# A decoder trunk on one core: VectorE turns the first mixer's latent queries, and SyncE issues the transfers of turned queries and keys

## The chip, the core and the metric

The kernel runs on one core of one Trainium2 chip. A core has TensorE (PE, matrix products), VectorE (DVE), ScalarE (ACT), GpSimd (POOL) and SyncE (SP), which issues transfers; GpSimd issues some too. The metric is the time of one execution in device microseconds (us); lower is better.

## What is computed

Two layers over 256 positions of width 1024, each a half-step feed-forward block, a mixer with three attention branches, and a second half-step block. Of the mixer, the latent attention matters here:

```python
q = (rms_norm(c_q, q_norm) @ w_uq).reshape(B, S, 8, 64 + 32)
kv = (rms_norm(c_kv, kv_norm) @ w_ukv).reshape(B, S, 8, 64 + 64)
k = concatenate([k_nope, broadcast(k_r)], -1)
q, k = rms_norm(q, gain_q), rms_norm(k, gain_k)
q = concatenate([q[..., :64], rope(q[..., 64:], pos)], -1)   # k likewise
o_mla = causal_attention(q, k, v)                            # 8 heads of 96
...
y = gate0 * (o_sb @ proj_sb) + gate1 * (o_mla @ proj_mla) + gate2 * (o_nsa @ proj_nsa)
x = x + y @ w_out
```

The other branches are a stick-breaking attention (sb) and a sparse attention (nsa), each with 8 heads too.

## The kernel before

All products are float32 in three passes: each operand is split into a rounded part and a rest (`hi` and `lo`), and TensorE does hi x hi, hi x lo and lo x hi (`mm3`, lines 588 to 590). Weights stream from memory in slabs of 128 x 1024. In a mixer `weights()` (lines 1017 to 1049) loads each of the 69 slabs in one of two ways: as two raw tiles, which ScalarE rounds (L1042) and VectorE subtracts (L1044); or, for slabs that the feed-forward block before has already split and put into memory (`early`), as four loads of finished halves (L1030, tiles `whi` and `wlo`). 10 slabs of the first mixer and 20 of the second come that way. Four slabs have room at once (`W_BUFS`), and six raw tiles (`RAW_BUFS`). All these loads are issued by SyncE, one after the other.

Inside a mixer, generators (one for each step of each branch) ask a `Planner` for engine time with estimated costs; it picks the request that could start first (with fixed offsets, `HOLDS` and `URGENCY`) and so writes down the order of TensorE, VectorE and ScalarE (`tc.manual_schedule`, lines 383 and 991). That order is kept on the chip. The order of SyncE and of GpSimd is left to the framework, which arranges each queue's instructions by its own model of when they are ready; on the chip a queue is then worked off in that order, and an instruction that waits holds up those behind it.

The latent queries and keys must stand with the 96 head dimensions on partitions before the scores. Two ways are in the code, chosen for queries (index 0) and keys (index 1) by `by_dve` (line 1260):

- TensorE: four transposes per pair of heads into a bank of the accumulator memory (lines 1707 to 1713), 16 in all.
- VectorE: `turn` (lines 1242 to 1249) transposes each 32 x 32 block of a 128 x 768 tile in place (L1245) and sends the tile in four transfers, one for each 32 partitions, to the memory tile `md` (L1247). It runs once for each half of the positions (t = 0, 1). For each pair of heads `turned` (lines 1251 to 1257) then reads three groups of 32 head dimensions back into a half tile `st` (L1255). The planner allows 6 us for the first transfers to land (line 1249) and 5 us for the second (line 1701).

Before the change, `by_dve` is `l in (1,), l in (0, 1)`: layer 0 turns its queries on TensorE and its keys on VectorE, layer 1 turns both on VectorE. `mla_T` then splits `st`, or the accumulator bank, on ScalarE and VectorE into `qk` tiles (lines 1068 and 1070), from which `mla_scores` computes the scores (lines 1731 to 1734, recorded at lines 588 to 590 as `att<-qk`). The reads of a pair may start four slabs before its scores are due, the splits two (`MLA_AT`, the gates in lines 1699, 1705, 1707 and 1725). `nsa_T`, which overwrites the buffers of the turned tiles, waits for the last of `mla_T`'s TensorE transposes (`ev_mqk`) where one of the two goes by TensorE, and for the four `turn`s where both go by VectorE (line 1890).

Half tiles (`th`, 7 of them) are shared by `st`, gates, and several steps of the other branches. SyncE also issues `zc` (L1402), a small rearranging transfer of the sparse branch, in the middle of each mixer.

Of the kernel before, what the change touches and what calls it, by code (L numbers as in the profile page):

```python
# [17 lines left out]
S = 256  # L18
# [353 lines left out]
def decoder_trunk(ctx, tc, xt_in, wts, lcon, cst, out, depth=DEPTH):  # L372
    nc = tc.nc
# [20 lines left out]
    def big_tile(name, dt=F, shape=(128, D)):  # L394
        return hp.tile(list(shape), dt, tag="hy", name=name, bufs=6)
# [552 lines left out]
    def mixer(l):  # L948
# [14 lines left out]
        def half_tile(name):  # L963
            return mp.tile([128, 512], F, tag="th", name=name, bufs=TH_BUFS)
# [277 lines left out]
        def turn(x, t, dst, n, k):  # L1242

            k = yield "V", 0.065 + 0.00116 * n, 0.15 + 0.00116 * n, (k,), ()
            nc.vector.transpose(x[:, 0:n], x[:, 0:n])  # L1245
            for i in range(4):
                nc.gpsimd.dma_start(dst[:, :, t * 128 + 32 * i:t * 128 + 32 * (i + 1)],  # L1247
                                    x[32 * i:32 * (i + 1), 0:n].rearrange("b (m a) -> b m a", a=32))
            return Tok(k.t + 6.0)

        def turned(dst, parts):

            st = half_tile("st")
            for r, m, step, c in parts:
                nc.gpsimd.dma_start(st[32 * r:32 * (r + 1), c * S:(c + 2) * S].rearrange("b (j n) -> b j n", j=2),  # L1255
                                    dst[:, m:m + step + 1:step, :])
            return st

        mq = [big_tile("mq", F, (128, 768)) for _ in range(NT)]
        by_dve = l in (1,), l in (0, 1)  # L1260
        md = [dp.tile([32, 24, S], F, tag=f"md{i}", name="md") if by_dve[i] else None for i in range(2)]
        mk = [big_tile("mk", F, (128, 768)) for _ in range(NT)]
        ev_mq, ev_mk, ev_V1 = events(NT), events(NT), events(NT)
# [36 lines left out]
        def mla_q_norm(t, ks):  # L1300
            x = mq[t].rearrange("p (h d) -> p h d", h=8)
            k = yield use_a(768, *ks, slots=(s_tmp,))
            sq = tmp()
            nc.scalar.activation(sq, mq[t], AF.Square)
            k = yield use_v(768, k)
            ss = sm.tile([128, 16], F, tag="ss", name="ss")
            nc.vector.tensor_reduce(ss[:, 0:8], sq.rearrange("p (h d) -> p h d", h=8), axis=AX.X, op=OP.add)
            s_tmp.put(k)
            k = yield use_v1(8, k)
            r = rstd(ss, 1.0 / 96, w=8)  # L1310
            k = yield use_g(2.5, k)
            k = yield use_v(768, k)
            nc.vector.tensor_tensor(x, x, r[:, 0:8, None].to_broadcast([128, 8, 96]), op=OP.mult)
            yield "-", 0.0, 0.0, (), (s_wf,)
            b = wf()[:, 0:256].rearrange("p (h d) -> p h d", h=8)
            k = yield from t_rope(x[:, :, 64:96], x[:, :, 64:96], tab["mq"], t, 8, 32, b, k)
            s_wf.put(k)
            if by_dve[0]:
                k = yield from turn(mq[t], t, md[0], 768, k)
            ev_mq[t].set(k)  # L1320
# [19 lines left out]
        def mla_k_norm(t, ak, k):  # L1340
# [28 lines left out]
            if by_dve[1]:  # L1369
                k = yield from turn(mk[t], t, md[1], 768, k)  # L1370
# [322 lines left out]
        def mla_T():  # L1693
            for p in range(4):
                srcs = (mq, ev_mq), (mk, ev_mk)
                st, land = [None] * 2, [None] * 2
                for i, (src, ev) in enumerate(srcs):
                    if by_dve[i]:
                        k = yield "-", 0.0, 0.0, (*ev, gate(MLA_AT, p, -4)), (s_th,)
                        st[i] = turned(md[i], [(e, 6 * p + e, 3, 0) for e in range(3)])  # L1700
                        land[i] = Tok(k.t + 5.0)
                T = []
                for i, (src, ev) in enumerate(srcs):
                    if by_dve[i]:
                        k = yield "-", 0.0, 0.0, (land[i], gate(MLA_AT, p, -2)), (s_qk, s_qk)
                    else:
                        k = yield use_t(4, *ev, gate(MLA_AT, p, -2), slots=(s_tp, s_qk, s_qk))
                        st[i] = tp_tile()
                        for j in range(2):
                            for t in range(NT):  # L1710
                                h = 2 * p + j
                                nc.tensor.transpose(st[i][:96, (2 * j + t) * 128:(2 * j + t + 1) * 128],
                                                    src[t][:, h * 96:(h + 1) * 96], ident)
                    if p == 3 and i == 1:
                        ev_mqk.set(k)
                    q = qk(), qk()
                    k = yield from t_split(q[0][:96], q[1][:96], st[i][:96], 512, k)
                    (s_th if by_dve[i] else s_tp).put(k)
                    T.append(q)
                    Tm[p] = T  # L1720
                    ev_Tm[p][i].set(k)
# [442 lines left out]
    for l in range(depth):  # L2164
        ffn(l, 0)
        mixer(l)
        ffn(l, 2)
# [35 lines left out]
```

## Time and profile before

| What | us |
| --- | --- |
| median of 3 runs (range) | 1248.34 (1248.22 to 1251.82) |
| the profiled execution | 1249.25 |
| its span, first to last instruction | 1247.4 |
| first mixer, first to last projection matmul | 186.6 to 422.2 |
| second mixer, likewise | 805.2 to 1041.2 |

Rows of the profile give the line of the kernel, the engine, the operation, the tiles as out<-in, and for groups the number of instructions, their busy time or their shortest, median and longest duration in ns. In a timeline the two first columns are start and duration in us, and a bracket at the end says how long the engine was idle before and what released it. SPq and POOL rows of DMA instructions are the time in which the queue is held by issuing; the time to landing is counted from the start of the issue. A matmul's end is modelled, so TensorE's true pace is read from the starts of neighbours.

### The profile page before, as it was taken

Reading aid. Unit: us, or ns where it says so; the run is one execution under the profiler, and the core shown is the slowest. Engines: PE = TensorE matmul, PEld = TensorE weight load, DVE = VectorE, ACT = ScalarE, POOL = GpSimd, SP = SyncE. Lnnn points to the kernel's source line nnn. Section 1 sums busy time; section 2 is a strip of 40 time slices with the busy share of each in tenths; the row PEclk is TensorE's granted clock in tenths of the full one; section 3 lists DMA queues with packets and bytes.
Section 4 is the critical chain, followed back from the end, with each engine's and each line's share of the span. In section 5 each row is a group of like instructions: output and inputs, shape, how many; then the busy total and the mean of one; then the engine's idle time right before and its main releaser. Section 6 shows DMA issues by size and latency. Waiting matters only on the chain.

```text
span 1247.4 us, 26169 instructions
## 1 busy us (share of the span) xinstructions
PE 1239.0 (99%) x9314; PEld 1158.8 (93%) x9314; DVE 943.6 (76%) x1961; ACT 789.0 (63%) x1633; POOL 155.5 (12%) x250
## 2 busy tenths in 40 slices
PE   9999999999999999999999999999999999999998
PEld 8999999888878899999999999998888889999987
DVE  7876668988898777766677776689968987776644
ACT  6665557787887566655465565577757775565542
POOL 0021201231000001211001121013330000023000
PEclk9999999999999999999999999999999999999999
DMA  8899985667645568999758999666896556677753
GB/s 273 288 328 327 334 270 184 196 209 245 207 126 182 158 218 260 319 322 339 233 196 272 330 328 324 213 211 191 280 323 236 159 157 185 189 211 244 220 169 119
DMA packets 157218, 298.59 MB, mean 239 GB/s; under 512 B 21472, under 2 KB 24416, under 8 KB 157088
## 3 DMA queue, kind: packets, MB, share of 16 engines
q1 hardware_dynamic: 143872, 258.64, 64.8%
q0 software_dynamic: 13216, 38.29, 8.4%
q8 instruction: 73, 1.20, 0.4%
q14 instruction: 57, 0.47, 0.1%
HBM read 258.32 MB, written 38.01 MB: 238 GB/s over the span
## 4 chain that ended last, share of the span: by engine, by line
PE 94%; ACT 2%; DVE 2%; DMA 1%; issue 1%; SPq 0%; DVEq 0%; ACTq 0%
PE acc L779 13%; PE acc L778 13%; PE acc L780 12%; PE acc L588 9%; PE acc L590 9%; PE acc L589 9%; PE acc L669 6%; PE acc L670 6%; PE acc L668 6%; PE acc L1204 1%; PE acc L1206 1%; PE acc L1205 1%; DMA raw<-in_wts 1%; PE att L2036 1%; ACT wf L1632 1%; PE tp L2047 1%
## 5 line engine op out<-in xcount | busy, mean ns | idle before, releaser
L536 DVE TENSOR_TENSOR vlo<-raw,vhi 128x512 fp32r<-128x512 f32 x452 | 292.6, 686 | 82.6 <-ACT vhi L535 80.4
L778 PE MATMUL acc<-hThi,vhi 128*128 128x256 f32 x1280 | 353.4, 276 | 0.0
L780 PE MATMUL acc<-hThi,vlo 128*128 128x256 f32 x1280 | 353.4, 276 | 0.0
L779 PE MATMUL acc<-hTlo,vhi 128*128 128x256 f32 x1280 | 353.4, 276 | 0.0
L535 ACT ACTIVATE vhi<-raw 128x512 fp32r<-128x512 f32 x452 | 263.5, 622 | 134.9 <-DMA raw<-in_wts 36.0
L778 PEld LDWEIGHTS acc<-hThi,vhi 128*128 128x128 f32 x1280 | 240.3, 188 | 0.0
L780 PEld LDWEIGHTS acc<-hThi,vlo 128*128 128x128 f32 x1280 | 240.2, 188 | 0.0
L779 PEld LDWEIGHTS acc<-hTlo,vhi 128*128 128x128 f32 x1280 | 240.2, 188 | 0.0
L1044 DVE TENSOR_TENSOR wlo<-raw,whi 128x512 fp32r<-128x512 f32 x216 | 141.1, 680 | 30.4 <-ACT whi L1042 28.7
L1042 ACT ACTIVATE whi<-raw 128x512 fp32r<-128x512 f32 x216 | 124.8, 616 | 47.6 <-PE acc L590 17.2
L670 PE MATMUL acc<-gh,vlo 128*128 128x256 f32 x528 | 145.7, 276 | 0.0
L668 PE MATMUL acc<-gh,vhi 128*128 128x256 f32 x528 | 145.7, 276 | 0.0
L669 PE MATMUL acc<-gl,vhi 128*128 128x256 f32 x528 | 145.7, 276 | 0.0
L588 PE MATMUL acc<-whi,hThi 128*128 128x512 f32 (+2 forms) x352 | 138.1, 392 | 0.0
L590 PE MATMUL acc<-whi,hTlo 128*128 128x512 f32 (+2 forms) x352 | 133.6, 380 | 0.2 <-DVE hTlo L610 0.2
L589 PE MATMUL acc<-wlo,hThi 128*128 128x512 f32 (+2 forms) x352 | 133.3, 379 | 0.0
L554 ACT ACTIVATE ehi<-eraw 128x512 fp32r<-128x512 f32 x60 | 37.9, 632 | 107.3 <-DMA eraw<-in_wts 105.1
L536 DVE TENSOR_TENSOR wlo<-raw,whi 128x512 fp32r<-128x512 f32 (+2 forms) x109 | 70.0, 678 | 45.7 <-ACT whi L535 45.5
L555 DVE TENSOR_TENSOR elo<-eraw,ehi 128x512 fp32r<-128x512 f32 x60 | 41.4, 690 | 81.0 <-ACT ehi L554 80.8
L535 ACT ACTIVATE whi<-raw 128x512 fp32r<-128x512 f32 (+2 forms) x109 | 63.1, 617 | 57.9 <-PE acc L590 26.4
L668 PEld LDWEIGHTS acc<-gh,vhi 128*128 128x128 f32 x528 | 99.1, 188 | 0.0
L669 PEld LDWEIGHTS acc<-gl,vhi 128*128 128x128 f32 x528 | 99.1, 188 | 0.0
(348 smaller groups left out, 2560.1 us busy)
## 6 DMA issues: line engine op xcount, KB each, us to landing
raw<-in_wts SPq DMA_DIRECT2D x764, 256.0 KB, 3.6
eraw<-in_wts SPq DMA_DIRECT2D x60, 256.0 KB, 5.5
early<-ehi POOLq DMA_DIRECT2D x60, 256.0 KB, 4.2
early<-elo POOLq DMA_DIRECT2D x60, 256.0 KB, 4.8
whi<-early SPq DMA_DIRECT2D x60, 256.0 KB, 4.4
wlo<-early SPq DMA_DIRECT2D x60, 256.0 KB, 4.6
st<-md POOLq DMA_DIRECT2D x36, 64.0 KB, 5.1
xd<-x SPq DMA_DIRECT2D x4, 512.0 KB, 2.6
```

Of the source, the lines that this page charges most:

```text
L535: nc.scalar.activation(hi[:, q], raw[:, o:o + g], AF.Copy)
L536: last_lo[0] = nc.vector.tensor_tensor(lo[:, q], raw[:, o:o + g], hi[:, q], op=OP.subtract).ins
L588: nc.tensor.matmul(o, a[0], b[0], start=start, stop=False, **kw)
L589: nc.tensor.matmul(o, a[0], b[1], start=False, stop=False, **kw)
L590: nc.tensor.matmul(o, a[1], b[0], start=False, stop=stop, **kw)
L668: nc.tensor.matmul(o, sl[0][:, w], h, start=k == 0 and c == 0, stop=False)
L669: nc.tensor.matmul(o, sl[0][:, w], l_, start=False, stop=False)
L670: nc.tensor.matmul(o, sl[1][:, w], h, start=False, stop=k == kts - 1 and c == 1)
L778: nc.tensor.matmul(o, sl[0][:, w], h, start=k == 0 and c == 0, stop=False)
L779: nc.tensor.matmul(o, sl[0][:, w], l_, start=False, stop=False)
L780: nc.tensor.matmul(o, sl[1][:, w], h, start=False, stop=k == KT - 1 and c == 1)
L1044: nc.vector.tensor_tensor(hl[1][:, c:c + m], raw[:, :m], hl[0][:, c:c + m], op=OP.subtract)
```

## The change

Layer 0 takes the VectorE path for its queries too, so in both layers queries and keys go through `turn` and `turned`; and all transfers of these two functions are issued by SyncE. The tile `md0` now exists in both layers, TensorE's 16 transposes of `mq` are gone, and `nsa_T` of layer 0 waits for the `turn`s in place of `ev_mqk`. For each mixer that makes 16 writes to `md` and 24 reads into `st` on SyncE's queue; before, GpSimd issued 8 and 12 of them in layer 0, 16 and 24 in layer 1. The planner is run anew with the same costs and offsets.

```diff
             nc.vector.transpose(x[:, 0:n], x[:, 0:n])
             for i in range(4):
-                nc.gpsimd.dma_start(dst[:, :, t * 128 + 32 * i:t * 128 + 32 * (i + 1)],
-                                    x[32 * i:32 * (i + 1), 0:n].rearrange("b (m a) -> b m a", a=32))
+                nc.sync.dma_start(dst[:, :, t * 128 + 32 * i:t * 128 + 32 * (i + 1)],
+                                  x[32 * i:32 * (i + 1), 0:n].rearrange("b (m a) -> b m a", a=32))
             return Tok(k.t + 6.0)
...
             for r, m, step, c in parts:
-                nc.gpsimd.dma_start(st[32 * r:32 * (r + 1), c * S:(c + 2) * S].rearrange("b (j n) -> b j n", j=2),
-                                    dst[:, m:m + step + 1:step, :])
+                nc.sync.dma_start(st[32 * r:32 * (r + 1), c * S:(c + 2) * S].rearrange("b (j n) -> b j n", j=2),
+                                  dst[:, m:m + step + 1:step, :])
             return st
...
-        by_dve = l in (1,), l in (0, 1)
+        by_dve = True, True
```

## The prediction

> **What bounds the kernel now.** The page first, for the engine whose work is the time; then the busy time of both mixers side by side, since the change touches only them.
>
> ```profile
> span 1247.4 us, 26169 instructions
> PE 1239.0 (99%) x9314; PEld 1158.8 (93%) x9314; DVE 943.6 (76%) x1961; ACT 789.0 (63%) x1633; POOL 155.5 (12%) x250
> PE 94%; ACT 2%; DVE 2%; DMA 1%; issue 1%; SPq 0%; DVEq 0%; ACTq 0%
> ```
>
> ```profile
> core 0: us, PE busy (x) PEld busy (x) DVE busy (x) ACT busy (x) POOL busy (x), PEclk, DMA share, GB/s
> 186.60:422.20 235.60, 234.86 (x1417) 200.64 (x1417) 206.80 (x523) 181.90 (x435) 28.04 (x31) 1.00 0.61 188
> 805.20:1041.20 236.00, 233.70 (x1401) 199.49 (x1400) 199.70 (x512) 171.09 (x411) 38.68 (x51) 1.00 0.69 217
> ```
>
> TensorE is busy 99% of the span and is 94% of the chain that ended last, at full clock in both mixers. So a change can win only TensorE work that goes, or TensorE idle time that closes; and it loses whatever makes TensorE wait in its fixed order. The two windows run from the first to the last projection matmul of each mixer. Layer 1 already turns queries and keys on VectorE; layer 0 turns only the keys so. Layer 1 has 16 matmuls fewer, exactly the transposes the change removes, yet it takes 0.4 us more: its TensorE idles 2.30 us (236.00 - 233.70), layer 0's 0.74. That is the nearest thing to a trial of the first half of the change, and it says: no gain. (Layer 1 also has more weights split ahead, so it is not a clean trial.)
>
> **The transposes.** Four groups of four, one per pair of heads, between projection matmuls; the row of the tile and one group in the timeline (start, duration):
>
> ```profile
> L1712 PE MATMUL tp<-ident,mq x16: 270/272/276, 278.1 to 317.1; 128*96 128x128 f32 x16
> ```
>
> ```profile
> 277.92 0.39 PE L590 MATMUL acc<-whi,hTlo 128*128 128x512 f32 x1
> 278.15 0.60 PE L1712 MATMUL tp<-ident,mq 128*96 128x128 f32 x4
> 278.50 0.48 PE L588 MATMUL acc<-whi,hThi 128*128 128x512 f32 x1
> 278.82 0.39 PE L589 MATMUL acc<-wlo,hThi 128*128 128x512 f32 x1
> ```
>
> The 272 ns each overlap; what counts is the delay of the neighbours. Projection matmuls follow each other every 0.23 us (277.92 to 278.15, where the group begins in L588's place). Without the group, L589 would start at 277.92 + 2 x 0.23 = 278.38; it starts at 278.82. So a group costs 0.44 us, four cost 1.75 us, all on the path: **-1.75 us**.
>
> **What replaces them in layer 0** is what layer 1 does now: two VectorE block transposes, 8 writes to the DRAM tile md and 12 reads back into st. The chain behind the last turn of layer 1, to the first scores, from the timelines of the engines:
>
> ```profile
> 891.72 0.97 DVE L1245 STREAM_TRANSPOSE mk<-mk 128x768 f32<-128x768 f32 x1
> 892.99 2.88 POOL L1247 DMA_DIRECT2D md<-mk  x4 [0.43 <-DVE mk L1245]
> 901.60 1.61 POOL L1255 DMA_DIRECT2D st<-md  x3 [5.74 <-ACT kd L1888]
> 908.21 0.63 ACT L1068 ACTIVATE qk<-st 96x512 fp32r<-96x512 f32 x1 [2.31 <-DMA st<-md]
> 908.01 0.28 PE L590 MATMUL acc<-whi,hTlo 128*128 128x256 f32 x1
> 908.89 0.33 PE L588 MATMUL att<-qk 96*128 96x128 f32 x1 [0.60 <-ACT qk L1068]
> 909.61 0.33 PE L589 MATMUL att<-qk 96*128 96x128 f32 x1 [0.40 <-DVE qk L1070]
> 914.57 0.39 PE L590 MATMUL acc<-whi,ol 128*128 128x512 f32 x1
> 915.64 0.33 PE L1673 MATMUL tp<-ident,wf 128*128 128x128 f32 x1 [0.68 <-ACT wf L1664]
> ```
>
> The turn ends at 892.69, the split of the read data starts at 908.21: 15.5 us, while the kernel's planner allows 6 + 5 (lines 1249 and 1701). TensorE waits: 0.76 us before the first score matmul (0.12 us is a neighbour's normal step), 0.60 before the second, 0.84 before the transposes of the probabilities: 2.2 us, nearly all of layer 1's idle time. This chain has no slack, so its changes arrive one for one.
>
> ```profile
> whi<-early SPq DMA_DIRECT2D x16, 256.0 KB, 5.1
> wlo<-early SPq DMA_DIRECT2D x16, 256.0 KB, 5.3
> raw<-in_wts SPq DMA_DIRECT2D x4, 256.0 KB, 4.6
> md<-mk POOLq DMA_DIRECT2D x8, 96.0 KB, 4.5
> st<-md POOLq DMA_DIRECT2D x12, 64.0 KB, 5.6
> zc<-wf SPq DMA_DIRECT2D x4, 64.0 KB, 4.3
> ```
>
> ```profile
> st<-md POOLq DMA_DIRECT2D x9, 64.0 KB, 3.0
> md<-mk POOLq DMA_DIRECT2D x4, 96.0 KB, 2.6
> ```
>
> These are the transfers issued in 871 to 907 (layer 1) and, in the second fence, two kinds of those in 252 to 288 (layer 0), with the median time to landing. In layer 0 a write and a read land 1.9 + 2.6 = 4.5 us sooner, more than the 2.2 us that layer 1 is late by. The new stall in layer 0 lies between 0 and 2.2 us; I take **+0.7**, nearer to nothing for that reason. VectorE's two turns are 1.94 us on an engine that is 88% busy there (206.80 of 235.60); bounds 0 and 1.9, with the planner's new order of layer 0 in it (without the transposes it may put other steps earlier, worth -0.5 to +1); I take **+0.4**, since VectorE's 12% of free time covers most of it. Where that cover is gone, the weight splits queue behind the turn, and TensorE behind them.
>
> **The move to SyncE.** Per mixer 16 writes and 24 reads go from GpSimd's queue, where nothing urgent stands behind them, to the queue that loads all weights, in order. Its prices:
>
> ```profile
> L514 SPq DMA_DIRECT2D raw<-in_wts x494: 327/328/1557, 192.6 to 1040.5; - x165
> L1402 SPq DMA_DIRECT2D zc<-wf x8: 593/608/699, 267.4 to 890.4; - x8
> L1030 SPq DMA_DIRECT2D whi<-early x16: 327/404/1069, 870.7 to 905.0; - x16
> L1030 SPq DMA_DIRECT2D wlo<-early x16: 319/355/583, 871.1 to 905.5; - x16
> L1247 POOL DMA_DIRECT2D md<-mk x16: 692/740/789, 248.9 to 895.1; - x16
> L1255 POOL DMA_DIRECT2D st<-md x36: 533/536/605, 271.9 to 924.8; - x36
> ```
>
> No row shows SyncE issuing an md write. By the code it consists of 32 x 24 = 768 runs of 128 bytes; a raw load has 128 runs and holds SyncE 0.328 us; zc, the only transfer here with short runs (64 partitions x 4), has 256 and holds it 0.608. If the hold goes by the instruction, md costs 0.33; if by the run, 0.608 + 512 x (0.608 - 0.328) / 128 = 1.73. I take 1.2, half-way up from zc, the nearest row. An st read has 64 runs, at most 0.33.
>
> The Trainium skill ("Perfetto Trace Analysis", section "DMA Instruction — HWDGE (DVE, Sync)") says that the profiled window of a SyncE DMA covers the generation of all its descriptors, after which SyncE is free. By that rule the per-run end is the true one; the sum would be 1.6 us higher. The raw and zc rows agree in direction; two points don't prove a line.
>
> Layer 1's chain then changes by: the fourth write starts 3 x (1.2 - 0.74) = 1.4 us later (ends: 1.2 earlier, 3.0 later); it lands like weight loads of the same queue, 5.2 instead of 4.5 (+0.7); the reads land in 5.2 instead of 5.6 and the third starts 0.4 sooner (-0.8); SyncE is in the middle of something when the turn ends (0 to 2, I take 0.4). **+1.7 us**, ends -2.2 (no more stall can close) and +5. In layer 0 the same 1.7 is eaten by the 4.5 us above. GpSimd's small powers (rs) lose their DMA neighbours; TensorE waits for none of them, so nothing.
>
> **Who stands behind on SyncE.** The weights. An md write waits for its VectorE turn and a read for its md writes to land and a free half tile; while SyncE waits there, no weight is loaded. How much of that is free:
>
> ```profile
> 885.57 0.32 SPq L1030 DMA_DIRECT2D wlo<-early  x1
> 887.44 3.62 SPq L1402 DMA_DIRECT2D zc<-wf  x4
> 891.41 0.34 SPq L514 DMA_DIRECT2D raw<-in_wts  x1
> ```
>
> ```profile
> 898.09 0.58 SPq L1030 DMA_DIRECT2D wlo<-early  x1
> ```
>
> ```profile
> DMA to landing us min/median/max: 5.0/6.3/6.4
> ```
>
> ```profile
> 907.06 0.28 PE L588 MATMUL acc<-whi,hThi 128*128 128x256 f32 x1
> ```
>
> From 885.89 to 891.41 SyncE issues no weights because of zc, and TensorE does not stall: 5.5 us are covered by the slabs loaded ahead. The three views after that follow one slab: its last load is issued at 898.09 and lands, as the slowest of its four, by 904.5 (898.09 + 6.4); the slab is first used at 907.06: 2.6 us to spare. A turn's four writes at 1.2 hold SyncE 4.8 us: covered, **0**.
>
> **The sum**: -1.75 + 0.7 + 0.4 + 1.7 = +1.05 us. The profiled execution takes 1249.25 us (1.85 around its span) and becomes 1250.3; it is 0.91 above the median of the runs shown, 1248.34, so I forecast **1249.4**. Its own range, from the ends above without the worst together: 1246.5 to 1252.
>
> **Rivals.**
>
> *SyncE becomes the bound (slower).* In 871 to 907 SyncE issues 16 x 0.404 + 16 x 0.355 + 4 x 0.328 + 4 x 0.608 = 15.9 us of 36. The change adds 12 reads (4.0), one wait for md's landing (5.2) and 8 writes. At 1.2 this makes 34.7, at 1.73 it makes 38.9: over 36 from 1.36 us a write on, and then weights fall behind. Locally: four writes (6.9) with the wait for their landing (5.2) before the first read block weights for 12.1 us in layer 1 and 6.9 + 2.6 = 9.5 in layer 0; 5.5 of each is covered, so 6.6 + 4.0 - 1.75 = +8.9 at most, half of it where loads slip in between. About 1255, up to 1257. For it: the zc row, and the 2.6 us of spare. By the rule of the Trainium skill cited above, which gives the per-run price, this rival is the outcome. Against it: SyncE can be given another order by the framework than turn, write, read in one block.
>
> *All hidden (faster).* Writes at 0.33, SyncE free at the right times, landing no later: the 2.2 us of stall close too, -1.75 - 2.2 = -3.95 at best, 1244.4; with some stall left in layer 0, 1245.5. For it: the read's shorter issue. Against it: the mixers' rows above, and md's many runs.
> The Trainium skill ("SBUF — State Buffer", section "SBUF: two separate sides") says that GpSimd's DMA issue is starved while VectorE runs its two-port modes, and that a SyncE DMA is not; that would favour this rival. This trace shows no starving: the md issues stay within 692 to 789 ns beside a VectorE at 85 to 88%.
>
> That the change doesn't act is excluded: line 1260 alone decides layer 0's path.
>
> **How the numbers follow.** About 0.3%, 3.75 us, is what a measurement can tell from no change: 1244.6 to 1252.1. Forecast 0.50 (0.47 within, 0.03 above); SyncE bound 0.38, all above; all hidden 0.12 (0.05 below, 0.07 within). So faster 0.05, same 0.54, slower 0.41. Cases of both signs hold the chance; the range takes the hidden case with some stall left and SyncE's full price: 1246 to 1258.
>
> **What would show it.** Right: no L1712, TensorE 16 matmuls fewer; SyncE's md rows near 1.2 us; layer 1's wait before the first score near 3 us instead of 1.4, and no wait for weights. Wrong: md rows at 0.6 or below with that wait gone (hidden), or TensorE, or ScalarE's weight splits, waiting several us for `whi`, `wlo` or `raw` right after md writes on SyncE (bound). A stall in layer 0 over 2.2 us would mean that its new order, not SyncE, is dear.

## The result, and the profile after

The changed kernel takes 1257.89 us (median of 6 runs, 1254.89 to 1259.76), the kernel before, run beside it, 1248.97 (6 runs, 1247.61 to 1251.82): ratio 1.0069, 95% interval 1.0057 to 1.0082. It is 0.7% slower. That lies inside the range of the prediction, at its upper end; the likeliest case, no change at 1249.4, did not come. Why the range held is told below; it was not for the reasons that set it.

The profiled execution is the fastest of the six, 1254.89 us. What it shows is 5.7 us of span; the other five runs lost up to 4.9 us more, at a mean TensorE clock of 0.996 to 0.998 against its 0.999.

The page of the changed kernel, the same lines as in the prediction:

```profile
span 1253.1 us, 26134 instructions
PE 1238.7 (99%) x9298; PEld 1158.7 (92%) x9298; DVE 947.4 (76%) x1970; ACT 787.0 (63%) x1626; POOL 120.4 (10%) x190
PE 91%; DMA 4%; ACT 2%; SPq 1%; DVE 1%; issue 0%; ACTq 0%
```

The 16 transposes are gone (9314 - 16 = 9298 matmuls), and transfers have come onto the chain of waits: DMA 4% where it was 1%, TensorE 91% where it was 94%. The busy time of the engines in both mixers, from the first to the last projection matmul, as before:

```profile
186.40:430.10 243.70, 235.50 (x1401) 200.33 (x1400) 209.60 (x530) 179.02 (x427) 15.74 (x11) 0.99 0.61 188
812.70:1046.90 234.20, 233.01 (x1400) 199.29 (x1400) 198.06 (x508) 169.57 (x409) 15.82 (x11) 1.00 0.70 218
```

The second column is the length. The first mixer takes 243.7 us, 8.1 more; the second takes 234.2, 1.8 less. Outside the two windows 0.6 us is gained. So the two halves of the kernel answered with opposite signs, and the loss is TensorE's idle time in layer 0: 243.70 - 235.50 = 8.20 us, where it was 0.74. What TensorE waited for, from the waits of the whole span (us in total, times, longest):

```profile
PE acc L1518 <- ACT wr L1060: 3.7, 1, 3.7
PE tp L1673 <- ACT wf L1664: 1.7, 2, 1.2
PE tp L1673 <- DVE wf L1662: 1.4, 1, 1.4
```

Of the second row 0.5 us lies in layer 1; the rest of these, and a wait of 0.8 us for `zc` at L1804, is layer 0's. Two things are new there: 3.7 us before the product of the fourth pair with the values (L1518), and 1.2 + 1.4 us before transposes of probabilities (L1673).

Layer 1's chain behind its last turn, from the timelines of VectorE, SyncE, ScalarE and TensorE:

```profile
898.58 0.97 DVE L1245 STREAM_TRANSPOSE mk<-mk 128x768 f32<-128x768 f32 x1
899.68 2.73 SPq L1247 DMA_DIRECT2D md<-mk  x4
904.69 0.32 SPq L1255 DMA_DIRECT2D st<-md  x1
913.15 0.63 ACT L1068 ACTIVATE qk<-st 96x512 fp32r<-96x512 f32 x1 [0.35 <-DMA st<-md]
915.03 0.23 PE L588 MATMUL att<-qk 96*128 96x128 f32 x1
```

From the turn's end at 899.55 to the split it is 13.6 us where it was 15.5, and the waits of TensorE at the first scores are gone. One row of the issues says why the forecast of this chain was wrong (shortest, median and longest hold of SyncE in ns):

```profile
L1247 SPq DMA_DIRECT2D md<-mk x16: 561/642/1509, 261.3 to 901.7; - x16
```

An md write holds SyncE 0.64 us, not 1.2, and less than it held GpSimd (0.74).

### The profile page after: what moved, and what is told of

It reads as the page before. It is cut to its first block, busy times and chain, and to the rows that moved or that the text cites. A ratio compares the mean times of both kernels' runs of the same rounds, so it can differ in the third digit from the quotient of the medians.

```text
span 1253.1 us, 26134 instructions
## 1 busy us (share of the span) xinstructions
PE 1238.7 (99%) x9298; PEld 1158.7 (92%) x9298; DVE 947.4 (76%) x1970; ACT 787.0 (63%) x1626; POOL 120.4 (10%) x190
## 4 chain that ended last, share of the span: by engine, by line
PE 91%; DMA 4%; ACT 2%; SPq 1%; DVE 1%; issue 0%; ACTq 0%
PE acc L780 12%; PE acc L778 12%; PE acc L779 12%; PE acc L588 9%; PE acc L590 8%; PE acc L589 8%; PE acc L670 6%; PE acc L668 6%; PE acc L669 6%; DMA wlo<-early 3%; PE acc L1204 1%; PE acc L1205 1%; PE acc L1206 1%; PE att L2036 1%; ACT wf L1632 1%; DMA whi<-early 1%
## 5 line engine op out<-in xcount | busy, mean ns | idle before, releaser
L780 PEld LDWEIGHTS acc<-hThi,vlo 128*128 128x128 f32 x1280 | 240.4, 188 | 0.0
L590 PE MATMUL acc<-whi,hTlo 128*128 128x512 f32 (+2 forms) x352 | 133.5, 379 | 0.0
L670 PEld LDWEIGHTS acc<-gh,vlo 128*128 128x128 f32 x528 | 99.1, 188 | 0.0
```

The costliest lines, as they stand in the source:

```text
L590: nc.tensor.matmul(o, a[1], b[0], start=False, stop=stop, **kw)
L670: nc.tensor.matmul(o, sl[1][:, w], h, start=False, stop=k == kts - 1 and c == 1)
L780: nc.tensor.matmul(o, sl[1][:, w], h, start=False, stop=k == KT - 1 and c == 1)
```

## The experiments

Two theories stood after the result. Order: with VectorE turning the queries of layer 0 the planner writes another order for TensorE, VectorE and ScalarE there, and that order is worse. SyncE: the transfers and the weights get in each other's way on one queue. The experiments below separate them. The mixers' lengths in the tables are taken from the profiled execution of each kernel; the medians are beside runs of the kernel before at 1248.61 to 1248.97.

### VectorE's turns alone

```diff
-                nc.sync.dma_start(dst[:, :, t * 128 + 32 * i:t * 128 + 32 * (i + 1)],
+                nc.gpsimd.dma_start(dst[:, :, t * 128 + 32 * i:t * 128 + 32 * (i + 1)],
...
-                nc.sync.dma_start(st[32 * r:32 * (r + 1), c * S:(c + 2) * S].rearrange("b (j n) -> b j n", j=2),
+                nc.gpsimd.dma_start(st[32 * r:32 * (r + 1), c * S:(c + 2) * S].rearrange("b (j n) -> b j n", j=2),
```

This is the changed kernel with all transfers back on GpSimd.

> Layer 0's queries turned by VectorE, all transfers still issued by GpSimd. Theory A (the planner's new order of layer 0 is dear: there the second key turn moves from 260.6 to 286.1 and the fourth pair's scores from 326.1 to 345.9): the first mixer stays near the 243.7 us that it takes after the change (235.6 before), the second goes back to about 236.0, the time is 7 to 10 us above before. Theory B (SyncE, by holding up weights and the sparse branch's zc, costs the time): the first mixer falls to 235 to 237 us, the time is within 1.5 us of before.

Measured: 1253.76 us, ratio 1.0037 [1.0024, 1.0050]. Its two mixers, and the waits of TensorE:

```profile
187.00:428.30 241.30, 235.69 (x1401) 201.03 (x1400) 210.29 (x531) 179.94 (x427) 39.08 (x51) 0.99 0.61 190
810.90:1047.60 236.70, 234.19 (x1401) 201.13 (x1400) 198.45 (x509) 170.10 (x409) 38.71 (x51) 0.99 0.68 216
```

```profile
PE acc L1518 <- ACT wr L1060: 3.7, 1, 3.7
PE att L588 <- ACT qk L1068: 1.9, 1, 1.9
```

The wait of 3.7 us is there without SyncE; the waits at L1673 are not. So more than half of the loss in layer 0 (5.7 of 8.1 us) comes with VectorE's turns, less than I had put there. Layer 1 keeps its wait at the first scores (`att<-qk`).

### SyncE's transfers alone

```diff
-        by_dve = True, True
+        by_dve = l in (1,), l in (0, 1)
```

This is the other half: queries of layer 0 by TensorE, all transfers on SyncE.

> Layer 0's queries stay on TensorE as before; SyncE issues all transfers of turned tiles. Theory A: the first mixer keeps its 235.6 us (plus or minus 1), the second takes the 234.3 us that it takes after the change (236.0 before), the time is 1 to 2.5 us below before. Theory B: the time is 4 to 8 us above before, with TensorE waits in the first mixer.

Measured: 1251.99 us (10 runs), ratio 1.0024 [1.0011, 1.0036]. Layer 0 takes 235.6 us, as before the change; layer 1 takes 238.7. The one wait that matters, and SyncE's timeline a little before it (start, duration of a group):

```profile
PE acc L588 <- DMA whi<-early: 2.1, 2, 1.9
```

```profile
929.74 0.44 SPq L1030 DMA_DIRECT2D wlo<-early  x1
930.30 2.51 SPq L1255 DMA_DIRECT2D st<-md  x4
932.91 0.36 SPq L1030 DMA_DIRECT2D whi<-early  x1
```

The wait at the first scores has gone, but a projection slab is late once, at 939.98 us, after four reads had taken SyncE for 2.5 us. Neither theory had this: layer 0 went as the theory of the order had it, but layer 1 did not get shorter, and the time rose by 3.3 us where that theory had it fall. So the SyncE half costs too, and the two halves add up to about what the change cost: 0.37% + 0.24% = 0.61% beside 0.69%.

### The writes alone

```diff
-                nc.sync.dma_start(st[32 * r:32 * (r + 1), c * S:(c + 2) * S].rearrange("b (j n) -> b j n", j=2),
+                nc.gpsimd.dma_start(st[32 * r:32 * (r + 1), c * S:(c + 2) * S].rearrange("b (j n) -> b j n", j=2),
...
-        by_dve = True, True
+        by_dve = l in (1,), l in (0, 1)
```

> As the run with SyncE alone (layer 0's queries on TensorE), but only the writes to md are issued by SyncE; the reads stay with GpSimd. What it asks is which half of the move shortens layer 1's chain. If the writes do (behind the last turn they land after 4.6 us from SyncE, 8.2 from GpSimd), the second mixer takes 234 us or less, the time is 1.5 to 3 us below before; if the reads do, the second mixer stays at 236 us and the time is that of before.

Measured: 1249.02 us (11 runs), ratio 1.0001 [0.9993, 1.0010]. Layer 1 takes 233.8 us, 2.2 less than before, layer 0 237.5, 1.9 more; TensorE's only long wait is one of 1.4 us for `zc` in layer 0 (L1804). The gain of 1.5 to 3 us that was expected with the shorter layer 1 did not come.

No wait for a projection slab is left. So it is SyncE's reads that make weights late in layer 1, and the writes that shorten its chain. The lateness does not come in every run: two runs below whose layer 1 reads are on SyncE have such a wait of 1.3 and 1.4 us (the first of the reads given back, and the added matmuls), the changed kernel's profile has 0.3.

### Another order by another offset

```diff
-                spawn(mla_q_norm(t, ks), 0.4)
+                spawn(mla_q_norm(t, ks), 0.0 if l == 0 else 0.4)
```

> The changed kernel, with one offset of the planner changed in layer 0 alone (the norm of the queries is held back by 0 in place of 0.4), so that the same work comes in another order. The planner's own account then ends the first mixer's TensorE work at 239.9 in place of 243.2 (240.2 before the change). Theory A: the first mixer takes 235 to 239 us, the time is 5 to 9 us below the changed kernel and within 2 us of before. Theory B: SyncE has the same transfers to issue, the first mixer stays above 241 us and the time 5 us or more above before.

Measured: 1260.32 us, ratio 1.0092 [1.0080, 1.0105]; layer 0 takes 248.3 us. The planner promised a better order and the chip gave a worse time:

```profile
PE tp L1804 <- DMA zc<-wf: 5.7, 1, 5.7
```

This cure failed, and the numbers are those that the theory of SyncE gave. `zc` is issued by SyncE, whose queue the planner's times leave out. The timelines of this run point to that queue: ScalarE had written the two inputs of `zc` (L1400) by 269.3 and 270.9 us, but SyncE issued `zc` only from 275.6 and 278.6 us on, behind four `md` writes that took it 5.7 us (one alone 3.6) and then three reads. No run gave the same order with `zc` issued early.

### Another order by the price of a turn

```diff
-            k = yield "V", 0.065 + 0.00116 * n, 0.15 + 0.00116 * n, (k,), ()
+            k = yield "V", 0.065 + 0.0008 * n, 0.15 + 0.0008 * n, (k,), ()
```

The instructions are those of the changed kernel; the planner is told a wrong price (a turn takes 0.97 us on the chip) and so writes another order. Once with all transfers on SyncE, once with GpSimd issuing everything but layer 1's writes:

> This is the changed kernel, instruction for instruction, with one number of the planner altered: it is told that a turn on VectorE costs 0.68 us in place of 0.96 (0.065 + 0.0008 x 768). The planner then puts the last turn of layer 0 at 84.3 of its own clock instead of 100.7, the scores of the fourth pair at 140.5 instead of 159.2, and promises 238.1 for layer 0 where it promised 243.2 (before the change 240.2). Theory order (the loss of the change lies in the order of layer 0 that the planner wrote, not in the work or in SyncE): the stall of 3.9 us before the last product with the values goes, and the half clock behind it; the mixer of layer 0 falls from 243.7 to 234 to 237 us and the kernel's time to 1246 to 1250. Theory work (VectorE's two turns more and SyncE's queue cost what was lost, in whatever order): the mixer of layer 0 stays at 241 to 244 and the time at 1254 to 1259.

> VectorE turns everything in both layers, the planner is told 0.68 us for a turn, GpSimd issues every transfer of layer 0 and the reads of layer 1, and SyncE issues the writes of layer 1 alone. Theory order: the cheap order of layer 0 without SyncE's transfers among the key blocks' own (mixer of layer 0 234 to 236 us), and the gain of SyncE's writes in layer 1 (mixer 233.5 to 234.5 against 236.0): 1244.5 to 1247, faster than both kernels by 2 us or more. Theory work: VectorE's turns cost in layer 0 as in the experiment with VectorE's turns alone (mixer 241): 1251 to 1253.

Measured: 1254.57 us on SyncE, ratio 1.0045 [1.0028, 1.0062]; 1248.98 us on GpSimd, ratio 0.9999 [0.9989, 1.0009]. Layer 0 of the first and of the second:

```profile
187.10:428.00 240.90, 235.48 (x1401) 199.85 (x1400) 208.41 (x524) 181.88 (x435) 15.54 (x11) 0.99 0.62 191
```

```profile
186.70:422.70 236.00, 234.10 (x1401) 198.77 (x1401) 208.57 (x524) 181.65 (x435) 39.08 (x51) 1.00 0.62 195
```

In neither is there a wait before the fourth product, so the order made that one. But by its length and its time the first went as the theory of the work had it: on SyncE layer 0 still takes 4.9 us more than on GpSimd, with a wait of 3.1 us at L1673 that the theory of the order did not expect:

```profile
PE tp L1673 <- ACT wf L1664: 3.1, 1, 3.1
```

The second has the short layer 0 that the theory of the order gave it, but a time 2 us above what it promised. The issues of the third pair's reads say where the wait on SyncE is from; SyncE's timeline (rows left out at the dots), then GpSimd's:

```profile
296.75 0.85 SPq L514 DMA_DIRECT2D raw<-in_wts  x2
301.76 0.80 SPq L1030 DMA_DIRECT2D whi<-early  x2
...
304.52 3.84 SPq L1255 DMA_DIRECT2D st<-md  x6
```

```profile
293.50 3.22 POOL L1255 DMA_DIRECT2D st<-md  x6
```

The reads of the third pair go out at 304.5 on SyncE and at 293.5 on GpSimd. Between 297.6 and 301.8 SyncE issues nothing: it stands at a weight load whose buffer TensorE has not yet released (`SPq L1030 <- PE acc L590`, 4.1 us the longest), and the reads stand behind it. This wait is the longest piece of the delay of 11.0 us; for the rest the reads stand behind the issues and shorter waits of the other loads.

### The reads given back

```diff
-                nc.sync.dma_start(st[32 * r:32 * (r + 1), c * S:(c + 2) * S].rearrange("b (j n) -> b j n", j=2),
+                (nc.gpsimd if l == 0 else nc.sync).dma_start(st[32 * r:32 * (r + 1), c * S:(c + 2) * S].rearrange("b (j n) -> b j n", j=2),
```

This is done in the kernel with the wrong price, for layer 0 alone; then, for both layers (`nc.gpsimd`), in the changed kernel with its own order.

> The changed kernel with the planner told 0.68 us for a turn, and with the reads of layer 0 alone (the 24 transfers st<-md) given back to GpSimd; SyncE keeps all 32 writes and layer 1's reads. Theory queue (on SyncE the reads of the third and fourth pair stand behind weight loads that wait for a buffer: 304.5 us where GpSimd issued them at 293.5): the reads go out before 297 us again, the scores of the fourth pair fall from 329.2 to about 324, the stall of 3.3 us at 311 goes, and the mixer of layer 0 takes 236 to 237.5 us instead of 240.9; time 1249 to 1251. Theory writes (what SyncE's transfers cost in layer 0 is the weights late behind the writes, and the wait for the turned blocks of the key): the mixer stays at 239.5 to 241, time 1253 to 1255.

> The changed kernel with all reads (st<-md of both layers) given back to GpSimd, and the planner's prices untouched, so the order of layer 0 is the change's own. Theory queue with theory order: the reads' part goes, the order's part stays: mixer of layer 0 241 to 242 us instead of 243.7 with the stall of 3.5 to 4 us before the fourth product with the values still there, layer 1 at 234 to 235; time 1253.5 to 1255.5. Theory writes: the mixer stays at 243 to 244, time 1256.5 to 1259. If the reads were all of it (no part for the order): mixer 235 to 237, time 1247 to 1249.

Measured: 1250.18 us (12 runs), ratio 1.0008 [0.9998, 1.0018], for the first; 1251.67 us (8 runs), ratio 1.0023 [1.0011, 1.0035], for the second. Layer 0 of each:

```profile
186.10:422.30 236.20, 233.91 (x1401) 198.62 (x1400) 208.50 (x524) 181.46 (x434) 28.34 (x35) 1.00 0.64 195
```

```profile
187.30:427.70 240.40, 235.54 (x1401) 201.17 (x1400) 210.80 (x532) 180.43 (x428) 28.61 (x35) 0.99 0.63 191
```

The first is as the queue theory had it; the reads of the third pair went out at 293.1 again. The second keeps the wait of 3.7 us at L1518 that belongs to the order, and loses the waits at L1673, again as it should; its layer 0 and its time came out a little below what was expected (240.4 for 241 to 242, 1251.7 for 1253.5 and more). Layer 0 in all, in us:

| | reads by GpSimd | reads by SyncE |
| --- | --- | --- |
| queries on TensorE, the order of before | 235.6 (writes by GpSimd), 237.5 (by SyncE) | 235.6 |
| all on VectorE, order with the price 0.68 | 236.0 (writes by GpSimd), 236.2 (by SyncE) | 240.9 |
| all on VectorE, the change's order | 241.3 (writes by GpSimd), 240.4 (by SyncE) | 243.7 |

So the change's 8.1 us are, along one path through the table, 0.6 (from 235.6 to 236.2, work moved in the better order) + 4.2 (order) + 3.3 (reads). The other path gives 2.8 for the order and 4.7 for the reads: 1.4 us go to one or the other by the path. Single profiles stand behind these lengths, and that of the changed kernel is its fastest run; the medians agree in sign (1254.57 to 1250.18 for the reads of layer 0 alone, 1257.89 to 1254.57 for the price alone). In size they differ. Four kernels have all writes on SyncE: from 1249.02 (queries on TensorE, reads by GpSimd) it is 2.7 us to 1251.67 (queries on VectorE, reads by GpSimd) and 6.2 more to 1257.89 (the change), or 3.0 to 1251.99 (queries on TensorE, reads by SyncE) and 5.9 more to the change. So both parts are shown, the turns with their order at 2.7 to 5.9 us and the reads at 3.0 to 6.2, and which of the two is the larger is not.

### The writes of layer 1 alone

The kernel before with one edit:

```diff
-                nc.gpsimd.dma_start(dst[:, :, t * 128 + 32 * i:t * 128 + 32 * (i + 1)],
+                (nc.sync if l == 1 else nc.gpsimd).dma_start(dst[:, :, t * 128 + 32 * i:t * 128 + 32 * (i + 1)],
```

> The kernel before, with the writes of layer 1 alone moved to SyncE; layer 0 is untouched. Theory chain (SyncE's writes shorten the chain behind layer 1's last turn by about 2 us, and in the experiment with the writes of both layers this was lost again to a wait for the turned blocks of the key in layer 0): mixer 235.6 in layer 0 and 233.8 in layer 1, 1246 to 1247.5, ratio 0.998 to 0.999. Theory chance (the shorter mixer of layer 1 in that run belonged to the shift of layer 0 and not to the issuing engine): layer 1 stays at 236 and the time at 1248.5 to 1249.

Measured: 1247.54 us (11 runs) beside 1248.61 (23 runs), ratio 0.9993 [0.9983, 1.0002]. Its second mixer, and the timelines of the chain:

```profile
804.40:1038.30 233.90, 232.92 (x1401) 199.43 (x1400) 198.81 (x510) 170.49 (x410) 28.65 (x35) 1.00 0.69 219
```

```profile
890.35 0.97 DVE L1245 STREAM_TRANSPOSE mk<-mk 128x768 f32<-128x768 f32 x1
891.34 2.68 SPq L1247 DMA_DIRECT2D md<-mk  x4
904.40 0.63 ACT L1068 ACTIVATE qk<-st 96x512 fp32r<-96x512 f32 x1
```

The chain takes 13.1 us (15.5 before) and the mixer 2.1 us less, as expected for the chain. The three other kernels with this division in layer 1 (writes by SyncE, reads by GpSimd) agree: their second mixers take 233.4 to 234.2 us. The kernel has the lowest median of all, but its profiled execution is the fastest of its 11; over the runs 1.1 us is left of the 2.1, and the interval reaches 1.0002: no faster kernel is shown.

### TensorE kept busy in its longest wait

The profile of the changed kernel shows a second loss behind the wait of 3.7 us. Busy times in steps of 2.5 us; the third number from the right is the granted clock:

```profile
355.00:357.50 2.50, 0.52 (x3) 0.35 (x3) 2.29 (x8) 2.45 (x8) 0.00 (x0) 0.93 0.37 105
357.50:360.00 2.50, 2.50 (x14) 2.50 (x15) 1.24 (x4) 1.09 (x3) 0.00 (x0) 0.50 0.39 111
360.00:362.50 2.50, 2.10 (x11) 1.60 (x10) 2.46 (x6) 1.66 (x4) 0.00 (x0) 0.89 0.00 0
```

If it is 1.00 or 0.50 at any time, the clock is halved for 0.07 x 5 of the first step, all of the second and 0.11 x 5 of the third: 0.35 + 2.5 + 0.55 = 3.4 us. The experiment puts 24 matmuls on constants into the wait:

```diff
                 oT = acc_tile()
+                if l == 0 and p == 3:
+                    for _ in range(24):
+                        nc.tensor.matmul(oT[:, 0:256], idR, sbm[:, 0:256], start=True, stop=True)
                 pv(oT, V1, (2 * p, 2 * p + 1), [[q[:, j] for q in Pm[p]] for j in range(2)])
```

> The changed kernel with 24 matmuls more in layer 0, ahead of the last product with the values, into the bank that this product then overwrites; they read constants, and 24 at 0.113 us are 2.7 us of TensorE inside its stall of 3.9 us. Theory clock (a stall of some 2 us or more makes the granted clock fall to a half for 3.4 us): the stall that is left is 1.2 us, the half clock behind it is gone, and the time falls by 1.7 us to about 1256 against 1257.9 of the changed kernel over all runs. Theory no link (the half clock comes from somewhere else): the clock falls at 357 us as before, time as the changed kernel's or up to 1 us more.

Measured: 1258.74 us, ratio 1.0076 [1.0063, 1.0089]; no gain. The clock in the same stretch, and the timeline of TensorE:

```profile
357.50:360.00 2.50, 1.82 (x15) 1.63 (x16) 1.72 (x4) 1.60 (x5) 0.00 (x0) 1.00 0.41 117
```

```profile
354.28 3.10 PE L1749 MATMUL acc<-rt 128*128 128x256 f32 x24
358.03 0.38 PE L1518 MATMUL acc<-wr,V 128*128 128x256 f32 x1 [0.65 <-ACT wr L1060]
362.15 0.50 PE L588 MATMUL acc<-whi,oh 128*128 128x512 f32 x1 [1.36 <-ACT oh L1068]
```

The half clock is gone, as the clock theory had it, but the 1.7 us did not come. From the fourth product to the next projection it is 362.15 - 358.03 = 4.1 us; in the changed kernel, at half clock, it is 4.5:

```profile
356.86 0.39 PE L1518 MATMUL acc<-wr,V 128*128 128x256 f32 x1 [3.74 <-ACT wr L1060]
361.36 0.50 PE L588 MATMUL acc<-whi,oh 128*128 128x512 f32 x1 [0.40 <-ACT oh L1068]
```

TensorE is faster and then waits longer (1.36 for 0.40 us) for `oh`, the product's output. So here the half clock cost about 0.4 us: the fourth pair's chain sets the pace, not TensorE.

## Why the prediction was right or wrong

That the time lies inside the range was luck. The upper end, 1258, stood for SyncE's full price of 1.73 us a write, and a write took 0.64. The measured loss is 8.9 us (1257.89 - 1248.97) where the sum gave 1.05, and it came from two terms that the sum had at +0.4 and at 0: the new order of layer 0, and what stands behind what on SyncE.

**The transposes, -1.75.** They went. That they are worth 1.75 us was not shown: even in the better order with GpSimd issuing, layer 0 takes 236.0 us, not 233.9. TensorE's busy time there is 0.8 us less than before (234.10 for 234.86), but its idle time is 236.00 - 234.10 = 1.9 us against 0.74, 1.2 us more: what is gained turns into waits, as the look at layer 1 had suggested.

**VectorE's turns and the new order, +0.4 (bounds -0.5 to 1.9): the first step that failed.** The order alone cost 2.8 to 4.2 us by the table (5.3 with GpSimd issuing all), above the upper bound of 1.9; by the medians the turns with their order cost 2.7 to 5.9. I had taken the new order for a matter of a microsecond because the turns themselves are 1.94 us of VectorE. But the turn's length is not what a new plan costs. The planner spread the two key turns of layer 0 from 13 us apart to 26, as the timeline of VectorE shows it grouped (first and last start; before, then after):

```profile
L1245 DVE STREAM_TRANSPOSE mk<-mk x2: 972/976/980, 247.6 to 260.6; 128x768 f32<-128x768 f32 x2
L1245 DVE STREAM_TRANSPOSE mk<-mk x2: 970/971/972, 260.3 to 286.1; 128x768 f32<-128x768 f32 x2
```

and put the split of the fourth pair's keys behind other work of VectorE. Its data had been read by then: the last four reads were issued from 318.8 us on and landed in at most 4.1 us, and the split ran at 344.0 (before the change the last one ran at 324.2).

```profile
L1255 SPq DMA_DIRECT2D st<-md x4: 371/428/435, 318.8 to 320.2; - x4
```

```profile
L1070 DVE TENSOR_TENSOR qk<-st,qk x1: 678/678/678, 344.0 to 344.0; 96x512 fp32r<-96x512 f32 x1
```

**The stall in layer 0, +0.7 (0 to 2.2).** 7.5 us of idle time came instead (8.20 - 0.74). The bound came from how late layer 1 is; layer 0 has another order and was late elsewhere. The prediction's last sentence said that a stall above 2.2 us would mean the order, not SyncE: that was half right, for by the table the reads on SyncE have 3.3 to 4.7 us of layer 0's loss.

**The md writes, 1.2 us each.** 0.64. SyncE's hold did not follow the number of runs: 768 runs cost 0.64 us where zc's 256 cost 0.61. A read of 64 runs, for which the prediction had 0.33 at most, held it 0.42 (median of 48). The rule of the Trainium skill ("Perfetto Trace Analysis", section "DMA Instruction — HWDGE (DVE, Sync)"), read as a price for each run, gave 1.73; the measurement is far below it. That reading was mine: the section names no price for a run.

**Layer 1's chain, +1.7 (ends -2.2 and +5).** In the profile it became about 2 us shorter, near the lower end. Two terms were wrong: the hold, and the landing, which I had put at that of weight loads (5.2). The last turn's writes land in 2.8 us at most on SyncE, and took up to 6.1 on GpSimd. The mixer did not always follow: three other runs have the change's layer 1 (SyncE alone, the other offset, the added matmuls), and it took 238.7, 235.7 and 236.0 us there, where the changed kernel's profile has 234.2.

**Who stands behind on SyncE, 0: the second step that failed.** For the writes this held: with writes alone no wait for weights is left. For the reads it did not: they made one slab late by 1.9 us where the halves were run apart. Above all the question was put one way only. I asked which weights stand behind the transfers, and not which transfers stand behind weights: a read that had its data by 293 waited until 304.5 behind loads whose buffers were not free. The chain of waits of the changed kernel shows the same at 310 us, under its own plan: a product of TensorE, the weight loads whose buffer it releases, the reads behind them, the split. With the reads by GpSimd and the same plan (the last row) those of the third pair go out at 303.6 us, not at 309.9:

```profile
308.65 0.24 PE acc L590
308.96 0.43 SPq L1030
309.44 0.42 SPq L1030
309.91 0.43 SPq L1255
310.38 0.42 SPq L1255
310.85 4.75 DMA st<-md
315.70 0.63 ACT qk L1068
```

```profile
303.60 3.16 POOL L1255 DMA_DIRECT2D st<-md  x6 [3.27 <-PE tp L1902]
```

**The rivals.** "SyncE becomes the bound" came nearest in time (1255 to 1257), but not by its mechanism: its point of decision was 1.36 us a write, and the write holds 0.64. "All hidden" had its sign in layer 1: md rows near 0.6 and the wait at the first scores gone, worth 1.8 of its 2.2 us. So in the profile layer 1 went as this rival had it, and layer 0 as none of the cases did.

What stays open: why the timed runs of the changed kernel lie 0.8 to 4.9 us above its profiled one. Their clocks are lower by 0.001 to 0.003, which fits more or longer waits of the kind above, and a layer 1 of up to 238.7 us in place of 234.2 would be a part of it; but only one of the six was profiled.

## What to carry to other kernels

A queue that works in order delays in both directions: before a transfer is moved to it, look not only at what will stand behind the transfer but at what the transfer will stand behind, above all loads that wait for a buffer to come free. Where a planner writes the order, removing a little work can cost more than the work, because a new order is drawn; compare the place of the last step of each chain in the two orders, and do not trust a promise that leaves a queue out. Undoing one half of a change at a time showed here that both halves lost and that one part of one half, the writes in layer 1, shortens that mixer by about 2 us, though no faster kernel came of it that is clear of the noise.

## What the runs showed of the hardware that was not expected

After TensorE had waited 3.7 us its granted clock was 0.50 for about 3.4 us, and in the run with VectorE's turns alone and in that with all reads by GpSimd for 6.8 us. A wait of 1.9 us was enough in layer 1 of the run with VectorE's turns alone, and in the run with SyncE's transfers alone; here are the two stretches behind the slab wait of the latter:

```profile
940.00:942.50 2.50, 2.36 (x6) 1.67 (x7) 0.73 (x3) 0.06 (x1) 0.00 (x0) 0.68 0.91 335
942.50:945.00 2.50, 2.50 (x16) 2.31 (x14) 0.82 (x2) 0.98 (x2) 0.00 (x0) 0.64 1.04 370
```

In the run with the added matmuls a wait of 2.0 us was not followed by it, and no wait of 1.5 us or less was. The Trainium skill ("TensorE: Matmul & The Clock Gate", section "HAM oscillation — how this bites in real kernels") names idle gaps over about 3.4 us as the limit, and a window of that length. The length of the half clock agrees (3.4 us and twice that); the limit does not, since 1.9 us was enough twice. Why a wait of 1.9 us was followed by the half clock and one of 2.0 us was not stays open.

The writes to `md` landed in 2.4 to 2.8 us when SyncE issued those behind layer 1's last turn, and in 3.8 to 6.1 when GpSimd did, with the same bytes; with nothing else moved (the writes of layer 1 alone) it was 2.3 to 2.4 us. This holds for that place and not everywhere: with the planner told 0.68 us SyncE's took 4.0 to 5.1 us there, and behind layer 0's last turn GpSimd's took 2.4 to 2.8 before the change. SyncE's hold for an md write, 0.64 us for 768 runs of 128 bytes, was hardly above its hold for `zc`.
